# A stick-breaking and forgetting attention block: three loads queued behind the transposing DMA, a second cast tile, and one low part computed ahead of the scan

## The chip, the cores and the metric

The kernel runs on one core of a Trainium2 chip. The metric is device time in microseconds (us) of one execution, as the median of three runs; one further execution was profiled. A core has TensorE (PE, matmul, and PEld for loading its weights), VectorE (DVE), ScalarE (ACT), GpSimd (POOL) and SyncE (SP), which here issues nearly all DMA transfers. Each engine works through its own instructions in order.

## What is computed

One layer of an encoder on a sequence of 512 rows and 2048 columns in float32:

- h = RMSNorm(x); one projection of h gives q, k, v for 16 heads of width 128, and forget gates.
- Eight heads use stick-breaking attention. With z = q k^T / sqrt(128), strictly causal, the weight of key s for query t is exp(log sigmoid(z) + the sum of log sigmoid(-z) over the keys between s and t). That sum is a reversed running sum along each row: a scan.
- Eight heads use forgetting attention: a softmax of z plus a cumulative log-forget bias ("fox" in the code).
- Each head's output o is normalized: o * rsqrt(mean(o^2) + eps) * g.
- x = x + heads @ W_out; x = x + relu(RMSNorm(x) @ W_up)^2 @ W_down; y = RMSNorm(x).

## The kernel before, in words

Every float32 operand of a matmul is split into a high part (rounded by a cast to fp32r on ScalarE) and a low part (the difference, on VectorE), and each product is made of three matmuls (`mm3`, L76 to L79). So each operand costs one cast, one subtraction and room for both parts.

The kernel has a first stage (norm, values), then the attention stage this text is about, then the output projection and the two matrices of the MLP. W_out, W_up and W_down are multiplied with a scheme of seven products, which needs sums of quarters of these matrices; the sums for W_out are made during the attention stage by class `WeightSums` (L952 to L988) and stored to DRAM.

The attention stage has 17 periods, n = 0 to 16, written out by hand as a list of jobs: `plan.at(t, f)` gives job f the time mark t, `plan.run()` calls the jobs in order of their marks, and in this order they stand on each engine. A mark is a place in an order, not a wait. A period has marks of 26.05 (TPER), t = TPER * n; "mark 13.6 of a period" is t + 13.6. In period n three heads are at work:

- Head n is projected: `project` (L205) in four parts, each over eight blocks of 128 rows of W_in, two for q and two for k. Their pieces of W_in (class `Piece`, 512 KB each, tile `wraw`, three in turn) are loaded, cast and subtracted; piece 3 is the last. A piece's tile is free again when its low part is made. Marks on TensorE: 0, 7.35, 14.8, and 20.3 with 23.4.
- Head n-1 has its scores (mark 5.45) and its weights: for fox heads bias, maximum, exponential and scaling; for stick-breaking heads (periods 9 to 16) `start`, `soft`, `maxed` with a causal select on POOL, `scan` (L815: four scans on VectorE and one subtraction), and `weights` (exponential on ScalarE, select on POOL). Then `halves` (L869) parts the upper and lower 16 bits on ScalarE, and `turn_halves` (L873) turns them by a transposing DMA issued from SyncE.
- Head n-2 has its transposed halves joined on ScalarE (`join_halves`, L877, mark 5.4), cast and subtracted (`t_high`, `t_low`), multiplied with the values (`product`, L896, mark 12.85), and normalized: `square` (three operations on ScalarE), `square_low` (L932, VectorE), `norm_sums` (L937 and L938, two matmuls with a matrix of ones on TensorE), `norm_1` (ScalarE), `norm_2` (four operations on VectorE).

Values are loaded for two heads at a time (`load_v`, tile `vr`, one of it), cast (`high_v`) and subtracted (`low_v`).

The sums for W_out come for eight row pairs m. `whole(m)` (m = 0 to 3, periods 1 to 7) loads both sides of a pair, 1 MB each, into a part of the tile `mixed`; `half(m, 0, n)` and `half(m, 1, n)` (m = 4 to 7, called for n = 7, 9, 11, 13 and n = 8, 10, 12, 14) load half of the columns at a time, 512 KB a side, into the one tile `ws`. The first half also has its quarters 0 and 2 cast by `high(i)` into a tile `tboth`, subtracted by `low(i)` and stored to DRAM (`wraws`), and a sixth sum by `high_6`, `low_6` (`whigh`). All three of these casts share the one tile tagged `thi`, so each must wait until the one before is stored. Casts and sums of half(m, 0, n) and half(m, 1, n) fall into period n + 1.

ScalarE, VectorE and TensorE keep this order through the whole stage. SyncE does so up to mark 55.05 only (`free_loads`, L724); after it the framework's planner, which goes by times that it estimates itself, places the transfers in SyncE's queue. The queue is in order: a transfer that has to wait holds all those behind it.

The marks that matter most, on VectorE and ScalarE in a stick-breaking period:

```
for dt, f in zip((12.85, 15.0, 21.7, 23.0, 23.4, 24.8) if late else (12.85, 17.1, 19.2, 20.25, 20.7, 22.05),
                 (H.product, H.square, H.square_low, H.norm_sums, H.norm_1, H.norm_2)):
    plan.at(t + dt, f)
```

(`late` is n > 8 here; the scan stands at 17.0.)

Of the kernel before, what the change touches and what calls it, by code (L numbers as in the profile page):

```python
# [37 lines left out]
def block_kernel(ctx, tc, x, g_attn, w_in, b_f, g_out_sb, g_out_fox, w_out, g_mlp, w_up, w_down, g_final, y):  # L38
# [118 lines left out]
    class Piece:  # L157
# [19 lines left out]
            lows[0] = dve.tensor_tensor(self.lo, self.source(), self.hi.bitcast(F32), op=ALU.subtract)  # L177

        def plan(self, plan, load, cast, low):
            plan.at(load, self.load)  # L180
            plan.at(cast, self.cast)
            plan.at(low, self.low)
            return self

    def q_piece(i, which, half):
        h = order[i]
        c0 = (o0 if h >= NH else 0) + h % NH * P + which * WSB
        return Piece(w_in[half * K8 * P:(half + 1) * K8 * P, c0:c0 + P].rearrange("(a p) c -> p a c", p=P), K8, P)
# [523 lines left out]
    with tc.tile_pool(name="att", bufs=1, side="right", reuse_waits="tile") as at, \  # L712
# [73 lines left out]
        class Head:  # L786
# [13 lines left out]
            def plan_sb(self, plan, t):  # L800
                g = self.h

                def start():
                    self.w = wide("w")
                    act.activation(self.w, self.s, AF.Abs)

                def soft():
                    act.activation(self.w, self.w, AF.Exp, scale=-1.0)
                    act.activation(self.w, self.w, AF.Ln, bias=1.0)

                def maxed():
                    dve.scalar_tensor_tensor(self.w, self.s, 0.0, self.w, op0=ALU.max, op1=ALU.add)
                    causal(self.w, ALU.is_gt, 0.0)

                def scan():  # L815
                    for r in rows(self.w):

                        dve.tensor_tensor_scan(r[:, ::-1], r[:, ::-1], r[:, ::-1], 0.0, op0=ALU.add, op1=ALU.max)
                    dve.tensor_tensor(self.w, self.s, self.w, op=ALU.subtract)

                def weights():
                    act.activation(self.w, self.w, AF.Exp)
                    causal(self.w, ALU.is_gt, 0.0)

                last_ = self.i == 2 * NH - 1
                for dt, f in zip((6.4, 7.7, 10.2, 14.5, 19.2) if last_ else (9.8, 11.0, 13.6, 17.0, 21.7), (start, soft, maxed, scan, weights)):
                    plan.at(t + dt, f)

            def plan_fox(self, plan, t):
# [42 lines left out]

            def turn_halves(self):  # L873
                self.two = wide("pl")
                sp.dma_start_transpose(self.two.bitcast(U16).rearrange("p (b t) -> p b t", t=P), self.one.bitcast(U16))

            def join_halves(self):  # L877
                self.pt = wide("pt")
# [65 lines left out]
            def norm_2(self):  # L944
# [4 lines left out]
                dve.scalar_tensor_tensor(va, sq, -3.0 * P, ra, op0=ALU.add, op1=ALU.mult)  # L949
                dve.scalar_tensor_tensor(mixed[:, self.h, :], self.os, gv, va, op0=ALU.mult, op1=ALU.mult)  # L950

        class WeightSums:  # L952

            def __init__(self, m, ds, place):
# [8 lines left out]
                    sp.dma_start(self.b[:, 2 * s:2 * s + 2], src[:, :, self.ds[0] * NT:self.ds[0] * NT + self.n])  # L963

            def high(self, i):
                self.both = at.tile([P, 2, NT], F32R, tag="thi", name="tboth")
                act.copy(self.both[:, 0], self.q[(0, 2)[i]][:, :NT])

            def low(self, i):
# [20 lines left out]
        def whole(m, t):  # L990
            w = WeightSums(m, (0, 1), lambda: mixed[:, :NH].rearrange("p (q a) n -> p q (a n)", a=2))
            e, o = (t, t + TPER) if m else (TPER, TPER)
            loads = (-4.0 if m == 1 else -15.0, 2.7) if m else (20.5, 20.6)
            highs, lows_, sums_, sixth = ((e + 3.3, o + 3.3), (e + 4.5, o + 4.5), (e + 6.4, e + 16.3, o + 6.4, o + 16.3), (o + 10.7, o + 20.6)) if m else \
                ((e + 4.0, e + 10.0), (e + 5.2, e + 11.0), (e + 6.4, e + 19.2, e + 20.6, e + 21.8), (e + 22.0, e + 24.0))
            for i in range(2):
                plan.at(t + loads[i], w.load, (i,))
                plan.at(highs[i], w.high, i)
                plan.at(lows_[i], w.low, i)
            for i in range(4):  # L1000
                plan.at(sums_[i], w.sum, i)
            plan.at(sums_[1] + 0.1, lambda: w.store(0, 2))
            plan.at(sixth[0], w.high_6)
            plan.at(sixth[1], w.low_6)
            plan.at(sixth[1] + 0.1, lambda: w.store(2, 4))

        def half(m, d, n):
            t = TPER * n
            w = WeightSums(m, (d,), lambda: at.tile([P, 2, 1280], F32, tag="ws", name="ws")
                           .rearrange("p a b -> p (a b)")[:, :4 * NT].rearrange("p (q n) -> p q n", q=4))  # L1010

            def load():
                with tc.issue_after(lows[0].ins):
                    w.load()

            if d == 0:
                jobs = [({7: 8.3, 9: 25.0}.get(n, 13.0), load if n == 7 else w.load)]
                a = (3.3, 4.5, 6.3, 6.35, 16.3, 10.7, 16.35, 20.6, 24.4, 24.9) if n == 7 else (4.3, 5.7, 6.4, 7.1, 7.8, 9.75, 11.3, 12.0, 14.7, 16.3)
                jobs += [(TPER + dt, f) for dt, f in zip(a, (lambda: w.high(0), lambda: w.low(0), lambda: w.sum(0), lambda: w.sum(1), lambda: w.sum(2),
                                                             lambda: w.high(1), lambda: w.low(1), lambda: w.sum(3), w.high_6, w.low_6))]  # L1020
                jobs += [(TPER + a[-1] + 0.1, w.store)]
            else:
                jobs = [(TPER + 3.0 if n == 8 else 20.5, w.load)]
                a = (11.3, 12.0, 16.3, 23.6) if n == 8 else (6.95, 7.65, 8.35, 9.05)
                jobs += [(TPER + dt, lambda j=j: w.sum(j)) for j, dt in enumerate(a)] + [(TPER + a[-1] + 0.1, w.store)]
            for dt, f in jobs:
                plan.at(t + dt, f)
# [22 lines left out]
        for n in range(2 * NH + 1):  # L1050
            t = TPER * n
            i_s, i_o = n - 1, n - 2
            if n < 2 * NH:
                pieces = []
                for a, (which, hf) in enumerate(((0, 0), (0, 1), (1, 0), (1, 1))):
                    if n == 0 and a < 3:
                        pieces.append(first_pieces[a])
                        continue
                    load = (-21.0, -15.0, -14.0, -2.0)[a]
                    if n == 0:  # L1060
                        cast, low, load = 16.3, 18.2, 0.3
                    elif n == 1:
                        cast, low = ((-7.0, -5.0), (-3.0, -2.0), (2.9, 3.9), (8.5, 9.5))[a]
                        load = (-23.0, -19.0, -13.1, -7.5)[a]
                    else:
                        cast, low = ((-12.35, -10.95), (2.3, 3.3), (3.9, 5.2), (9.7, 11.2))[a] if n <= NH else ((-9.25, -3.65), (2.3, 3.3), (3.3, 4.5), (13.6, 15.1))[a]
                        if a == 0 and n == NH + 1:
                            cast, low = -12.35, -10.95
                    pieces.append(q_piece(n, which, hf).plan(plan, t + load, t + cast, t + low))
                marks = [(0, 0, 8, 0.0), (1, 0, 8, 7.35), (2, 0, 8, 14.8), (3, 0, 4, 20.3), (3, 4, 8, 23.4)]  # L1070
                if n == 0:
                    marks = [(2, 0, 2, 16.2), (2, 2, 8, 17.6), (3, 0, 4, 21.6), (3, 4, 8, 24.3)]
# [23 lines left out]
            if 0 <= i_s < 2 * NH:  # L1096
                H = heads[i_s]
                plan.at(t + (5.45 if n < 2 * NH else 4.4), H.scores)
                sb = H.h < NH
                (H.plan_sb if sb else H.plan_fox)(plan, t)  # L1100
                if n < 2 * NH:
                    plan.at(t + (24.7 if sb else 22.0), H.halves)
                    plan.at(t + (24.8 if sb else 22.1), H.turn_halves)
                else:
                    tp = t + 1.45 * 14 + 1.95 - 0.05
                    plan.at(tp, H.turn)
                    plan.at(tp + 1.2, H.p_high)
                    plan.at(tp + 2.5, H.p_low)
                if i_s % 2 == 0 and i_s < 2 * NH - 2:
                    p_ = i_s // 2  # L1110
                    plan.at(t - 12.0 if p_ else t + 3.0, load_v, p_)
                    plan.at(t + (4.3 if sb else 11.3 if p_ else 12.0), high_v, p_)
                    plan.at(t + (5.7 if sb else 24.9 if p_ else 16.35), low_v, p_)
            if 0 <= i_o < 2 * NH - 1:
                H = heads[i_o]
                last_ = i_o == 2 * NH - 2
                for dt, f in zip((11.25, 13.6, 19.3) if last_ else (5.4, 8.5, 9.8), (H.join_halves, H.t_high, H.t_low)):
                    plan.at(t + dt, f)
                if last_:
                    continue  # L1120
                late = n > NH
                for dt, f in zip((12.85, 15.0, 21.7, 23.0, 23.4, 24.8) if late else (12.85, 17.1, 19.2, 20.25, 20.7, 22.05),
                                 (H.product, H.square, H.square_low, H.norm_sums, H.norm_1, H.norm_2)):
                    plan.at(t + dt, f)
        for i, dt in ((2 * NH - 2, 1.0), (2 * NH - 1, 3.0)):
# [979 lines left out]
```

## Time and profile before

| what | us |
|---|---|
| median of three runs | 2039.17 |
| lowest and highest of them | 2039.15, 2040.46 |
| the profiled execution's own time | 2042.29 |
| its span, first to last instruction | 2040.6 |
| TensorE busy in it | 2006.4 |
| granted TensorE clock, mean | 0.995 |
| period 3 (a fox period), from the first matmul of its projection to the next period's | 26.09 |

How to read the profile. Rows of a timeline give the start in us from the span's start, the duration, the engine, the line of the kernel, the operation and its tiles as output<-input; a bracket at the end gives the idle time of the engine before it and what ended that. The engine name SPq stands for SyncE's queue; the duration of a transfer there is that of issuing it, not of the transfer. Matmul durations overlap, as they are pipelined: TensorE starts one about every 0.23 us while a row shows 0.39. The chain of waits is followed back from the last instruction: what it shows are the steps that ended last. Rows of DMA issues give size and median time from issue to landing. The granted clock is 1.00 at full and 0.50 at half speed.

The periods' starts, from the timeline of TensorE (first projection matmul of each head): 200.68 (n = 2), 235.77, 261.86 and so on to 392.33 (n = 9), 418.42, 450.63, 478.98, 508.95, 541.75, 573.54 (n = 15), and 601.45, where the last values begin (n = 16).

### The profile page before, as it was taken

The numbers are of one execution on the slowest core, as the hardware profiler recorded it, in microseconds if no ns is written. First come the engines' busy times: TensorE is split into PE (matmuls) and PEld (weight loads), VectorE is DVE, ScalarE is ACT, GpSimd is POOL, SyncE is SP. The second block draws the span as 40 slices with busy tenths as digits, with TensorE's granted clock in tenths as the row PEclk, the third lists the DMA queues.
The fourth block names the chain that finished last, engine by engine and source line by source line (L and its number), as shares of the span: only waits on it lengthen the run. The fifth ranks groups of instructions, "written<-read, shape, count | busy, mean of one in ns | idle before, by whom it ended". The sixth has DMA issues, their size and how long they took to land.

```text
span 2040.6 us, 27057 instructions
## 1 busy us (share of the span) xinstructions
PE 2006.4 (98%) x10302; PEld 1734.9 (85%) x10302; DVE 1741.2 (85%) x1968; ACT 1201.0 (59%) x1645; POOL 63.6 (3%) x73
## 2 busy tenths in 40 slices
PE   9999899989999999999999999999999999999998
PEld 9998788877778889988888888888888888888887
DVE  7876788787677678899999999998799898888896
ACT  7544666767665566667676676676644444444344
POOL 0000000011010000000000000000000000000003
PEclk9999999999999999999999999999999999999999
DMA  7418877666668882576666667667685674674642
GB/s 257 155 63 255 263 231 213 206 197 183 179 180 277 272 279 95 176 225 191 213 195 209 200 197 221 187 207 258 228 297 207 221 253 175 236 254 173 225 159 89
DMA packets 309426, 423.54 MB, mean 208 GB/s; under 512 B 49408, under 2 KB 205104, under 8 KB 302768
## 3 DMA queue, kind: packets, MB, share of 16 engines
q1 hardware_dynamic: 308544, 419.71, 63.3%
q8 instruction: 81, 1.33, 0.3%
q10 hardware_dynamic: 752, 2.11, 0.3%
q14 instruction: 49, 0.40, 0.1%
HBM read 315.45 MB, written 96.49 MB: 202 GB/s over the span
## 4 chain that ended last, share of the span: by engine, by line
PE 89%; DVE 4%; DMA 3%; ACT 3%; issue 1%; SPq 0%; POOL 0%; ACTq 0%; DVEq 0%
PE psa L1277 11%; PE accd L79 8%; PE accd L78 8%; PE accd L77 8%; PE psa L1275 6%; PE psc L1277 5%; PE accq L77 3%; PE accq L79 3%; PE accq L78 3%; PE psc L1275 3%; PE psb L1277 3%; PE psb L1275 1%; PE m L78 1%; PE m L77 1%; PE m L79 1%; DMA wraws<-tboth 1%
## 5 line engine op out<-in xcount | busy, mean ns | idle before, releaser
L1913 ACT CAST wh<-wd 128x1024 fp32r<-128x1024 f32 x126 | 124.8, 998 | 169.3 <-PE accd L79 54.6
L1799 DVE TENSOR_TENSOR wl<-wu,wh 128x1024 fp32r<-128x1024 f32 x158 | 192.7, 1220 | 12.1 <-ACT wh L1793 12.0
L77 PE MATMUL accq<-hH,wh 128*128 128x512 f32 x512 | 201.7, 394 | 0.0
L79 PE MATMUL accq<-hH,wl 128*128 128x512 f32 x512 | 201.1, 393 | 0.3 <-DVE wl L177 0.3
L78 PE MATMUL accq<-hL,wh 128*128 128x512 f32 x512 | 200.8, 392 | 0.0
L1793 ACT CAST wh<-wu 128x1024 fp32r<-128x1024 f32 x158 | 167.6, 1061 | 44.1 <-issue 28.0
L1277 PE MATMUL psa<-f,wh 128*128 128x512 f32 x720 | 179.1, 391 | 0.0
L78 PE MATMUL accd<-wl,uf 128*128 128x512 f32 x436 | 169.7, 389 | 0.0
L79 PE MATMUL accd<-wh,uf 128*128 128x512 f32 x436 | 169.7, 389 | 0.0
L77 PE MATMUL accd<-wh,uf 128*128 128x512 f32 x436 | 169.6, 389 | 0.0
L1277 PEld LDWEIGHTS psa<-f,wh 128*128 128x128 f32 x720 | 132.4, 188 | 25.5
L1920 DVE TENSOR_TENSOR wl<-wd,wh 128x1024 fp32r<-128x1024 f32 x126 | 144.0, 1151 | 10.9 <-ACT wh L1913 10.9
L1913 ACT CAST wx<-wd 128x1024 fp32r<-128x1024 f32 (+1 forms) x82 | 80.8, 994 | 106.5 <-PE accd L79 41.9
L1634 DVE TENSOR_TENSOR m<-m,accd 128x1024 f32<-128x1024 f32 x84 | 102.2, 1217 | 46.3 <-PE accd L79 46.3
L79 PEld LDWEIGHTS accq<-hH,wl 128*128 128x128 f32 x512 | 96.8, 189 | 21.7 <-DVE wl L177 1.2
L78 PEld LDWEIGHTS accq<-hL,wh 128*128 128x128 f32 x512 | 97.0, 189 | 19.5
L77 PEld LDWEIGHTS accq<-hH,wh 128*128 128x128 f32 x512 | 97.2, 190 | 19.0
L77 PE MATMUL accd<-wx,uf 128*128 128x512 f32 x284 | 110.6, 389 | 0.0
L79 PE MATMUL accd<-wx,uf 128*128 128x512 f32 x284 | 110.6, 389 | 0.0
L78 PE MATMUL accd<-wx,uf 128*128 128x512 f32 x284 | 110.6, 389 | 0.0
L1275 PEld LDWEIGHTS psa<-f,wl 128*128 128x128 f32 x720 | 96.0, 191 | 5.3
L1275 PE MATMUL psa<-f,wl 128*128 128x256 f32 x720 | 98.3, 283 | 0.0
(443 smaller groups left out, 5135.3 us busy)
## 6 DMA issues: line engine op xcount, KB each, us to landing
wu<-in_w_up_dram SPq DMA_DIRECT2D x60, 1024.0 KB, 6.7
ufd<-st SPq DMA_DIRECT2D x98, 512.0 KB, 3.9
wd<-in_w_down_dram SPq DMA_DIRECT2D x48, 1024.0 KB, 8.7
uf<-ufd SPq DMA_DIRECT2D x42, 1024.0 KB, 8.0
wraw<-in_w_in_dram SPq DMA_DIRECT2D x68, 512.0 KB, 5.6
wo<-wsums SPq DMA_DIRECT2D x28, 512.0 KB, 4.5
q<-in_w_in_dram SPq DMA_DIRECT2D x32, 384.0 KB, 5.4
wd<-in_w_down_dram SPq DMA_DIRECT2D x16, 768.0 KB, 5.8
```

The lines of the kernel that those rows point to most:

```text
L77: pe.matmul(out, sh, mh, start=first, stop=False, skip_group_check=True)
L78: pe.matmul(out, sh, ml, start=False, stop=False, skip_group_check=True)
L79: return pe.matmul(out, sl, mh, start=False, stop=last, skip_group_check=True)
L1275: ins = pe.matmul(ps[:, 2 * P:], lo[:, a, :], f_parts(p, a)[0], start=False, stop=last, skip_group_check=True)
L1277: ins = pe.matmul(ps, hi[:, a, :], f_both(p, a), start=a == PAIRS[0] and p in (1, 5), stop=last, skip_group_check=True)
L1634: dve.tensor_tensor(M[p][:, :, db, :], M[p][:, :, db, :], ps, op=ALU.add)
L1793: act.copy(rooms[k][0], srcs[k])
L1799: lows[0] = dve.tensor_tensor(lo, srcs.pop(k), hi.bitcast(F32), op=ALU.subtract)
L1913: act.copy(rooms[k + 3][0], srcs[k + 3])
L1920: dve.tensor_tensor(rooms[k + 2][1], srcs.pop(k + 2), rooms[k + 2][0].bitcast(F32), op=ALU.subtract)
```

## The change

- `turn_halves` keeps its transposing DMA, and a new function `load_behind` issues a load inside `tc.issue_after(...)` of that DMA: the planner must place it in SyncE's queue behind the transposition. It is used for piece 3 of heads 3 to 15 (at t - 0.5 instead of t - 2.0) and for the load of the second halves of the W_out sums (mark 25.5 instead of 20.5, or 29.05 for n = 8).
- In the first halves the second cast `high(1)` goes into the tile of the value loads (`vr`) instead of `thi`. The value loads of stick-breaking periods stand at t - 7.0 instead of t - 12.0.
- In periods 9 to 16 `square_low` stands at 16.9, ahead of the scan, instead of 21.7, `norm_sums` at 20.25 instead of 23.0, `norm_1` at 20.7 instead of 23.4, ahead of `weights` (22.0 instead of 21.7), and `norm_2` at 24.4 instead of 24.8.
- The second halves' four sums stand at 8.35, 9.05, 11.3, 12.0 (before: 6.95 to 9.05, and 11.3 to 23.6 for n = 8). In period 8 the first half's third sum, second low part, last sum and sixth stand earlier; the load for n = 9 stands at 13.0 instead of 25.0.
- For m = 1 the first load stands at mark 0.5 of period 2 instead of 4.0 before it, its cast at 10.7 instead of 3.3, its low part at 11.15, and its first two sums at 16.3 and 24.9.

```diff
         def plan(self, plan, load, cast, low):
-            plan.at(load, self.load)
+            if load is not None:
+                plan.at(load, self.load)
...
                 last_ = self.i == 2 * NH - 1
-                for dt, f in zip((6.4, 7.7, 10.2, 14.5, 19.2) if last_ else (9.8, 11.0, 13.6, 17.0, 21.7), (start, soft, maxed, scan, weights)):
+                for dt, f in zip((6.4, 7.7, 10.2, 14.5, 19.2) if last_ else (9.8, 11.0, 13.6, 17.0, 22.0), (start, soft, maxed, scan, weights)):
...
-                sp.dma_start_transpose(self.two.bitcast(U16).rearrange("p (b t) -> p b t", t=P), self.one.bitcast(U16))
+                now["turn"] = sp.dma_start_transpose(self.two.bitcast(U16).rearrange("p (b t) -> p b t", t=P), self.one.bitcast(U16))
...
+        def load_behind(w):
+            with tc.issue_after(now["turn"].ins):
+                w.load()
...
             def high(self, i):
-                self.both = at.tile([P, 2, NT], F32R, tag="thi", name="tboth")
+                self.both = at.tile([P, 2, NT], F32R, tag="vr" if i and self.n == NT else "thi", name="tboth")
...
-            loads = (-4.0 if m == 1 else -15.0, 2.7) if m else (20.5, 20.6)
-            highs, lows_, sums_, sixth = ((e + 3.3, o + 3.3), (e + 4.5, o + 4.5), (e + 6.4, e + 16.3, o + 6.4, o + 16.3), (o + 10.7, o + 20.6)) if m else \
+            loads = (0.5 if m == 1 else -15.0, 2.7) if m else (20.5, 20.6)
+            highs, lows_, sums_, sixth = ((e + 3.3, o + 3.3), (e + 4.5, o + 4.5), (e + 6.4, e + 16.3, o + 6.4, o + 16.3), (o + 10.7, o + 20.6)) if m > 1 else \
+                ((e + 10.7, o + 3.3), (e + 11.15, o + 4.5), (e + 16.3, e + 24.9, o + 6.4, o + 16.3), (o + 10.7, o + 20.6)) if m else \
...
             if d == 0:
-                jobs = [({7: 8.3, 9: 25.0}.get(n, 13.0), load if n == 7 else w.load)]
-                a = (3.3, 4.5, 6.3, 6.35, 16.3, 10.7, 16.35, 20.6, 24.4, 24.9) if n == 7 else (4.3, 5.7, 6.4, 7.1, 7.8, 9.75, 11.3, 12.0, 14.7, 16.3)
+                jobs = [(8.3 if n == 7 else 13.0, load if n == 7 else w.load)]
+                a = (3.3, 4.5, 6.3, 6.35, 16.3, 10.7, 11.15, 17.0, 18.85, 20.6) if n == 7 else (4.3, 5.7, 6.4, 7.1, 7.8, 9.75, 11.3, 12.0, 14.7, 16.3)
...
             else:
-                jobs = [(TPER + 3.0 if n == 8 else 20.5, w.load)]
-                a = (11.3, 12.0, 16.3, 23.6) if n == 8 else (6.95, 7.65, 8.35, 9.05)
+                jobs = [(25.5, lambda: load_behind(w))]
+                a = (8.35, 9.05, 11.3, 12.0)
...
-                    pieces.append(q_piece(n, which, hf).plan(plan, t + load, t + cast, t + low))
+                    w = q_piece(n, which, hf)
+                    if a == 3 and n > 2:
+                        plan.at(t - 0.5, load_behind, w)
+                        load = None
+                    pieces.append(w.plan(plan, load and t + load, t + cast, t + low))
...
-                    plan.at(t - 12.0 if p_ else t + 3.0, load_v, p_)
+                    plan.at(t - (7.0 if sb else 12.0) if p_ else t + 3.0, load_v, p_)
...
-                for dt, f in zip((12.85, 15.0, 21.7, 23.0, 23.4, 24.8) if late else (12.85, 17.1, 19.2, 20.25, 20.7, 22.05),
+                for dt, f in zip((12.85, 15.0, 16.9, 20.25, 20.7, 24.4) if late else (12.85, 17.1, 19.2, 20.25, 20.7, 22.05),
                                  (H.product, H.square, H.square_low, H.norm_sums, H.norm_1, H.norm_2)):
```

## The prediction

> **What bounds the kernel now.** I read the page first, then the stretches, then chain, waits and timeline of the slow ones. The page:
>
> ```profile
> span 2040.6 us, 27057 instructions
> PE 2006.4 (98%) x10302; PEld 1734.9 (85%) x10302; DVE 1741.2 (85%) x1968; ACT 1201.0 (59%) x1645; POOL 63.6 (3%) x73
> PE 89%; DVE 4%; DMA 3%; ACT 3%; issue 1%; SPq 0%; POOL 0%; ACTq 0%; DVEq 0%
> ```
>
> TensorE is the bound; only time in which it stands still or runs at half clock can be won. The change lies in the attention part. I cut that at the first projection matmul (accq) of each head, as the timeline gives it, and asked for busy time in those stretches. Columns: stretch, length, busy PE, PEld, DVE, ACT, POOL, granted clock, DMA share, GB/s.
>
> ```profile
> core 0: us, PE busy (x) PEld busy (x) DVE busy (x) ACT busy (x) POOL busy (x), PEclk, DMA share, GB/s
> 200.68:235.77 35.09, 28.50 (x127) 23.89 (x125) 22.03 (x33) 17.61 (x24) 2.13 (x2) 0.90 0.90 274
> 235.77:261.86 26.09, 26.09 (x126) 22.11 (x125) 21.67 (x33) 18.73 (x25) 2.00 (x2) 1.00 0.74 227
> 418.42:450.63 32.21, 26.96 (x127) 22.02 (x125) 23.51 (x28) 20.61 (x22) 3.51 (x4) 1.00 0.72 217
> 450.63:478.98 28.35, 26.93 (x126) 22.03 (x125) 22.16 (x26) 20.20 (x20) 3.06 (x4) 1.00 0.79 231
> 478.98:508.95 29.97, 26.71 (x127) 21.96 (x125) 23.20 (x28) 20.98 (x22) 3.51 (x4) 1.00 0.58 168
> 508.95:541.75 32.80, 29.43 (x127) 24.53 (x125) 22.21 (x26) 20.64 (x20) 3.06 (x4) 0.90 0.74 197
> 541.75:573.54 31.79, 28.28 (x127) 23.10 (x125) 24.68 (x30) 21.92 (x22) 3.51 (x4) 0.95 0.52 149
> 573.54:601.45 27.91, 26.74 (x127) 22.03 (x125) 19.59 (x23) 17.86 (x18) 3.06 (x4) 1.00 0.63 175
> ```
>
> The second row (period 3) is clean: TensorE busy throughout, 26.09 us. Against it period 2 loses 9.00, and periods 10 to 15 lose 6.12, 2.26, 3.88, 6.71, 5.70 and 1.82: 35.5 us in all, clock dips included. That is the whole purse. Which waits fill it, by the list of waits of 180 to 640 us (total, times, longest) and the chain:
>
> ```profile
> PE ssq L938 <- DVE pl L932: 9.5, 3, 3.2
> ACT tboth L967 <- DMA wraws<-tboth: 17.2, 5, 6.3
> ```
> ```profile
> 452.05 7.26 DMA pl<-pt
> ...
> 486.04 6.57 DMA wraws<-tboth
> ...
> 510.39 9.27 DMA pl<-pt
> ...
> 573.40 8.38 DMA pl<-pt
> ```
>
> Three things end last: the norm sums on TensorE wait for `square_low`, which stands behind the scan (9.5 us, periods 10, 12, 14); the second `tboth` waits until the first is stored; and the transposing DMA at the end of the even periods takes 7.26, 9.27 and 8.38 us. SyncE's queue shows what the last meets, and the odd end at 480 shows it undisturbed:
>
> ```profile
> 449.14 1.21 SPq L963 DMA_DIRECT2D ws<-in_w_out_dram  x2
> 450.44 0.55 SPq L163 DMA_DIRECT2D wraw<-in_w_in_dram  x1
> 452.05 5.14 SPq L875 DMA_TRANSPOSE pl<-pt  x1
> ...
> 459.39 3.10 ACT L879 COPY pt<-pl 128x2560 uint16<-128x2560 uint16 x1 [2.86 <-DMA pl<-pt]
> ...
> 480.43 2.56 SPq L875 DMA_TRANSPOSE pl<-pt  x1
> ...
> 484.63 3.12 ACT L879 COPY pt<-pl 128x2560 uint16<-128x2560 uint16 x1
> ...
> 492.67 0.62 ACT L967 CAST tboth<-ws 128x512 fp32r<-128x512 f32 x1 [3.62 <-DMA wraws<-tboth]
> ...
> 505.11 0.68 DVE L932 TENSOR_TENSOR pl<-ph,pl 128x512 fp32r<-128x512 f32 x1
> ```
>
> Three loads of 512 KB go out in the 3 us before the slow transposition. The quick one has the join (L879) start 4.20 us after its issue, without a wait.
>
> **The change, part by part.** *Loads tied behind the transposition* (piece 3 of heads 3 to 15, the second half's two `ws` loads). They are the three in front of 452.05. What a transposition takes with loads behind it I bound from both sides: 4.2 us with none, and from a fox period with a 1 MB load right behind it:
>
> ```profile
> 260.22 2.53 SPq L875 DMA_TRANSPOSE pl<-pt  x1
> ...
> 262.84 0.53 SPq L963 DMA_DIRECT2D mixed<-in_w_out_dram  x1
> ...
> 265.74 3.11 ACT L879 COPY pt<-pl 128x2560 uint16<-128x2560 uint16 x1
> ```
>
> The join did not wait, so it had landed within 5.52. I take 4.85, the middle. By the Trainium skill, "DMA: Bandwidth & Descriptors", section "Two DMAs through the same engine are not ordered", descriptors of one queue start in order, so loads behind should cost nothing; by that it would be 4.2 and the sum below some 4 us better. A later load on its side: piece 3 is cast at mark 13.6 of its period, issued now near 3; hidden, and if it came 8 us later ScalarE's cast would hold the join loop us for us.
>
> *Second cast in the value tile.* The 3.62 us wait of period 12 goes (for m from 4; the whole pairs keep the one tile). The tile is needed for the value load only at mark 19 of the same period; that load moves from 12 to 7 ahead of its period, and its cast is at 4.3, eleven us later: nothing on the path.
>
> *`square_low` ahead of the scan.* VectorE's row of 0.68 now lies on the loop from join to next transposition. The join loop per pair of periods, by the rows above: odd, 459.39 to 480.43 = 21.04, plus 0.68 = 21.72; even, 484.63 to 510.39 = 25.76, less 3.62, plus 0.68 = 22.82; with two transpositions of 4.85 it is 54.24 against 52.18 of TensorE (52.94 at 4.2, 55.58 at 5.52). So the loop becomes the bound by 2.06 per pair, 6.2 in three pairs, less the slack it starts with. The slack: the join of period 12 comes 5.65 after the start and costs nothing, that of period 11 comes 8.76 after and costs
>
> ```profile
> 465.37 0.39 PE L78 MATMUL o<-pl,vh 128*128 128x256 f32 x1 [1.14 <-DVE pl L886]
> ```
>
> 1.14, so the limit is 7.6 and the slack 2.0. Left: 4.2 us (0.3 to 8.2).
>
> One rule speaks against this move. POOL's causal select runs just ahead of the scan:
>
> ```profile
> 498.71 2.14 POOL L778 TENSOR_SCALAR_AFFINE_SELECT w<-w 128x256 f32<-128x256 f32 x2 [20.67 <-DVE w L812]
> 506.63 1.37 POOL L778 TENSOR_SCALAR_AFFINE_SELECT w<-w 128x256 f32<-128x256 f32 x2 [5.78 <-ACT w L822]
> ```
>
> Beside VectorE's subtractions it takes 2.14, alone 1.37: they do slow one another, by 0.77. The Trainium skill, "SBUF — State Buffer", section "Who interferes with whom", has it that a VectorE instruction with two SBUF inputs and a GpSimd one that reads SBUF exclude each other for the whole instruction; `square_low` has two such inputs. By that rule up to 0.77 more per period would go onto the loop, six times, 4.6 us; by the rows two subtractions stand beside the select already, so I take nothing.
>
> *Norm sums and `norm_1` earlier.* TensorE now reaches the sums at mark 20.25 instead of 23. `square_low` would end where the scan of period 12 began, 4.6 us before 505.11, less 3.62, plus 0.68: 18.2 after 478.98. So 9.5 us of TensorE waiting go, with 2 us to spare; if the loop slips by more, the wait returns. The new wait: `norm_1` stands ahead of `weights` on ScalarE and waits for TensorE; behind it stand weights, select, halves, transposition. Sums done at 20.7, two activations of 0.65: 22.0; the scan's end is 23 in period 12 by the same reckoning, so 1 us of cover. `norm_2`, 0.4 earlier, stays last in its period: nothing.
>
> *The half pair's sums* (odd periods) move from 6.95–9.05 to 8.35–12.0, two ahead of `t_low`, two behind. Their `ws` loads now follow the transposition:
>
> ```profile
> ws<-in_w_out_dram SPq DMA_DIRECT2D x16, 512.0 KB, 5.2
> ...
> wsums<-ws SPq DMA_DIRECT2D x8, 1024.0 KB, 6.5
> ```
>
> Issued at 2.56 and 3.2 after the transposition's issue they land near 7.8 and 8.4; sums of 0.7 each end near 9.2, and `t_low` could begin at 4.85 + 3.12 + 1.27 = 9.2. Between nothing and 1.3 each; I take 0.5, 1.5 us in all. With the cover gone (a load that waits for the old tile's store first) each us late is a us lost. The first half's load of period 9 moves up 12 marks, and period 8's casts up 5.5: both off the path.
>
> *Pair 1's first load and casts* (period 2).
>
> ```profile
> 197.69 2.33 ACT L871 COPY pt<-w 128x2560 uint16<-128x2560 uint16 x1 [1.83 <-DVE w L856]
> ...
> 203.29 0.34 SPq L963 DMA_DIRECT2D mixed<-in_w_out_dram  x1
> 203.75 6.37 SPq L875 DMA_TRANSPOSE pl<-pt  x1
> 210.22 0.52 SPq L984 DMA_DIRECT2D whigh<-thi  x1
> ...
> 213.44 0.62 ACT L967 CAST tboth<-mixed 128x512 fp32r<-128x512 f32 x1 [8.64 <-DMA whigh<-thi]
> ...
> 214.91 3.04 ACT L879 COPY pt<-pl 128x2560 uint16<-128x2560 uint16 x1
> ```
>
> The halves are done at 200.02, the transposition goes out at 203.75 behind a waiting 1 MB load, the `whigh` store behind that, and a cast that waits for the store holds ScalarE until 213.44 and with it the join. Load and cast both move behind the join. Then: issue 200.05, landed by 205.6 (5.52), join 4.9 after the period's start, inside 7.6: all 9.0 come back. What is late next is the moved cast at mark 10.7, ahead of period 2's softmax; a miss of 2 us there meets the fox periods' slack.
>
> Sum: purse 35.5, less 4.2 (loop), less 1.5 (sums): 29.8. The profiled execution took 2042.29 (span 2040.6), 3.1 above the median of 2039.17; taking the gain from the median gives **2009.4**.
>
> **The rivals.** *Other loads slide in front.* After mark 55.05 SyncE's order is the planner's; only the named loads are tied. If untied pieces or stores precede the even transpositions, these keep their mean of 8.30: 57.69 per pair, 5.51 over, 16.5 in three, less 2.0, plus 1.5: gain 19.5, 2019.7. That is also the case that the ties do not do what they say. For it: stores of 1 MB a period pass the same queue; against: at 480.43 the order was clean.
>
> *`ws` late.* If these loads wait for a store and land 4 us later, VectorE holds `t_low` in three odd periods: 12 more, gain 17.8, 2021.4. For it: both halves share one tile; against: the store goes out at mark 16.4 and takes 6.5, done by 23.
>
> *Exclusion at the select*, as above: 4.6 more, 2014.0.
>
> *Slower.* The tie touches every head from 3 on. If the planner puts a load that waits (for a tile still being stored) between the transposition and piece 3, ScalarE's in-order queue holds cast, softmax and halves in each of 13 periods. It decides from 29.8 / 13 = 2.3 us a period; at 4 us, 2061. For it: in period 2 one waiting load on this queue cost 9 us; against: issued behind a fox period's transposition (260.22 + 2.53, 0.9 into its period) piece 3 has nearly 9 us until its cast at mark 9.7, where a load of its size takes 5.2.
>
> **How the numbers follow.** Forecast 55% (its own range 2003 to 2016: loop at its bounds), exclusion 10%, other loads 13%, `ws` late 10%, slower 9%, mishaps that cancel 3%. All but the last two are faster by over 0.2% (4 us; about what a measurement of this kernel can tell). The range runs from 2002 (the purse, and 1.7 for the neighbouring periods) to 2028 (above the two late cases).
>
> **What would show it.** Right: transpositions of periods 10, 12, 14 landing within 5.5 us, with `ws` and piece 3 issued behind; no wait of `tboth` for `wraws` from period 8 on; no wait of ssq for `square_low`; period 2 near 26. Wrong: joins later than 7.6 after the start, VectorE idle before the `ws` sums, ScalarE idle before `norm_1`. The forecast falls if the clean 26.09 of the fox periods grows, or if SyncE's order puts a waiting load ahead of the transposition.

## The result, and the profile after

The changed kernel takes 2012.23 us (median of four runs, 2011.52 to 2012.47) against 2039.81 of the kernel before in the same comparison (four runs, 2039.15 to 2040.46). The ratio is 0.9864, 95% interval 0.9847 to 0.9881: 27.6 us less, by the medians. The forecast was 2009.4, so direction and size came out. The profile shows that three terms of the sum did not, and that they nearly cancelled, which is luck.

The page of the changed kernel, the lines that answer to those of before (span; busy time; shares of the chain that ended last):

```profile
span 2010.4 us, 27058 instructions
PE 1997.9 (99%) x10302; PEld 1730.5 (86%) x10302; DVE 1738.8 (86%) x1968; ACT 1202.2 (60%) x1645; POOL 58.3 (3%) x73
PE 96%; DVE 1%; DMA 1%; ACT 0%; SPq 0%; issue 0%; ACTq 0%; DVEq 0%
```

TensorE's share of the chain went from 89% to 96%, and its busy time fell by 8.5 us although it runs the same 10302 matmuls. All of that lies in periods 10 to 15 (165.05 us busy before, 156.56 after, by the stretches), most of it in the two whose granted clock was 0.90 and 0.95 and is now 1.00. The profiled execution took 2012.10, which is the median almost to the tenth. Before, the profiled one stood 2.5 above its median.

The same stretches as in the prediction, cut again at the first projection matmul of each head (stretch, length, busy PE, PEld, DVE, ACT, POOL, granted clock, DMA share, GB/s). The last row is a part of the first:

```profile
core 0: us, PE busy (x) PEld busy (x) DVE busy (x) ACT busy (x) POOL busy (x), PEclk, DMA share, GB/s
200.78:232.01 31.23, 28.28 (x127) 23.21 (x125) 21.16 (x33) 17.36 (x23) 0.82 (x2) 0.95 0.86 262
232.01:258.10 26.09, 26.09 (x126) 22.11 (x125) 21.67 (x33) 18.74 (x25) 2.00 (x2) 1.00 0.79 252
414.66:440.76 26.10, 26.10 (x127) 22.11 (x126) 22.36 (x28) 20.65 (x22) 3.06 (x4) 1.00 0.72 217
440.76:466.85 26.09, 26.09 (x127) 22.11 (x125) 22.28 (x26) 20.77 (x20) 2.45 (x4) 1.00 0.74 227
466.85:492.94 26.09, 26.09 (x126) 22.11 (x125) 22.35 (x28) 20.67 (x22) 3.06 (x4) 1.00 0.74 217
492.94:519.04 26.10, 26.10 (x127) 22.11 (x125) 22.29 (x26) 20.78 (x20) 2.45 (x4) 1.00 0.74 227
519.04:545.13 26.09, 26.09 (x127) 22.11 (x125) 22.36 (x28) 20.64 (x22) 3.06 (x4) 1.00 0.65 197
545.13:571.22 26.09, 26.09 (x126) 22.10 (x125) 21.14 (x25) 19.80 (x19) 2.45 (x4) 1.00 0.68 206
224.00:228.00 4.00, 3.50 (x9) 2.73 (x9) 2.31 (x4) 2.61 (x4) 0.00 (x0) 0.58 0.05 14
```

Periods 10 to 15 (the six rows from 414.66) are all clean: the 26.49 us that they had lost came back whole. Period 2 (the first row) is 31.23 long and still loses 5.14 of its 9.00. The value stage n = 16 begins at 571.22 instead of 601.45, 30.23 earlier, and the span is shorter by 30.2: nothing else moved.

### The profile page after: what moved, and what is told of

It is laid out like the page before. It is cut to its first block, busy times and chain, and to the rows that moved or that the text cites. A ratio compares the mean times of both kernels' runs of the same rounds, so it can differ in the third digit from the quotient of the medians.

```text
span 2010.4 us, 27058 instructions
## 1 busy us (share of the span) xinstructions
PE 1997.9 (99%) x10302; PEld 1730.5 (86%) x10302; DVE 1738.8 (86%) x1968; ACT 1202.2 (60%) x1645; POOL 58.3 (3%) x73
## 4 chain that ended last, share of the span: by engine, by line
PE 96%; DVE 1%; DMA 1%; ACT 0%; SPq 0%; issue 0%; ACTq 0%; DVEq 0%
PE psa L1287 11%; PE accd L78 8%; PE accd L79 8%; PE accd L77 8%; PE psa L1285 6%; PE psc L1287 5%; PE accq L77 5%; PE accq L79 5%; PE accq L78 5%; PE psc L1285 3%; PE psb L1287 3%; PE psb L1285 1%; PE m L78 1%; PE m L77 1%; PE m L79 1%; PE accoa L79 1%
## 5 line engine op out<-in xcount | busy, mean ns | idle before, releaser
L77 PE MATMUL accq<-hH,wh 128*128 128x512 f32 x512 | 200.8, 392 | 0.0
L77 PE MATMUL accd<-wh,uf 128*128 128x512 f32 x436 | 169.4, 389 | 0.0
L1930 DVE TENSOR_TENSOR wl<-wd,wh 128x1024 fp32r<-128x1024 f32 x126 | 144.1, 1152 | 10.6 <-ACT wh L1923 10.6
L77 PEld LDWEIGHTS accq<-hH,wh 128*128 128x128 f32 x512 | 96.6, 189 | 19.0
L77 PE MATMUL accd<-wx,uf 128*128 128x512 f32 x284 | 110.5, 389 | 0.0
```

The costliest lines, as they stand in the source:

```text
L77: pe.matmul(out, sh, mh, start=first, stop=False, skip_group_check=True)
L1930: dve.tensor_tensor(rooms[k + 2][1], srcs.pop(k + 2), rooms[k + 2][0].bitcast(F32), op=ALU.subtract)
```

## What the queue and the loop look like now

SyncE's queue and the join at the start of period 11, from the timeline (start, duration, engine, line, operation, tiles; the idle time before it in brackets), and the median time of a transposition from issue to landing in 400 to 640 us, from the list of transfers:

```profile
441.67 2.55 SPq L876 DMA_TRANSPOSE pl<-pt  x1
444.31 1.21 SPq L968 DMA_DIRECT2D ws<-in_w_out_dram  x2
445.57 4.28 SPq L163 DMA_DIRECT2D wraw<-in_w_in_dram  x3
445.89 3.11 ACT L880 COPY pt<-pl 128x2560 uint16<-128x2560 uint16 x1 [0.28 <-DMA pl<-pt]
...
pl<-pt SPq DMA_TRANSPOSE x7, 4.2
```

The two `ws` loads and three pieces now go out behind the transposition, and the join starts 4.22 after its issue. The undisturbed transposition of before took 4.20. The loads behind it cost nothing that can be seen, where I had taken 4.85; the rule of the Trainium skill, "DMA: Bandwidth & Descriptors", section "Two DMAs through the same engine are not ordered" (descriptors of one queue start in order), would have put it at 4.2, and here the trace agrees with it.

Period 2, again by the timeline:

```profile
199.47 4.99 SPq L876 DMA_TRANSPOSE pl<-pt  x1
204.56 0.51 SPq L989 DMA_DIRECT2D whigh<-thi  x1
205.12 0.42 SPq L163 DMA_DIRECT2D wraw<-in_w_in_dram  x1
205.65 0.66 SPq L992 DMA_DIRECT2D wsums<-mixed  x1
206.40 0.46 SPq L968 DMA_DIRECT2D mixed<-in_w_out_dram  x1
206.63 3.12 ACT L880 COPY pt<-pl 128x2560 uint16<-128x2560 uint16 x1 [1.46 <-DMA pl<-pt]
...
215.42 0.62 ACT L972 CAST tboth<-mixed 128x512 fp32r<-128x512 f32 x1 [3.42 <-DMA mixed<-in_w_out_dram]
...
223.59 0.50 PE L938 MATMUL ssq<-pl,onesr 128*128 128x512 f32 x1 [2.45 <-ACT pl L930]
224.59 0.78 PE L939 MATMUL ssq<-pl,onesr 128*128 128x512 f32 x1 [0.50 <-DVE pl L933]
```

The transposition goes out at 199.47 instead of 203.75, near the 200.05 worked out. It takes 7.16 us and not 5.52, as a store of 1 MB (`wsums`, at 198.24) and 0.25 MB (`cb`, at 198.65) went out just ahead of it. The join starts at 206.63 instead of 214.91. But pair 1's cast (`tboth<-mixed`, mark 10.7) now waits 3.42 us on ScalarE for its 1 MB load, which is issued at 206.40 behind a store, a piece and a 1 MB store. The cast stands in ScalarE's order ahead of the softmax and the squares of the norm; these come late, and TensorE stands 2.95 us (2.45 + 0.50) at the norm sums. What follows runs at a granted clock of 0.58 from 224 to 228. Idle 31.23 - 28.28 = 2.95, and busy time 28.28 - 26.09 = 2.19 too long from the clock: 5.14.

## The experiments

In the expectations, theory A is the prediction's working, in which the ties carry most of what periods 10 to 15 win; theory B, its rival, gives the ties little. C and D ask of pair 1 whether the place of its cast or the order of the transfers is the cause. E and F stand for two readings of the norm part: E, that it is worth the waiting it takes away; F, that this waiting was only where a late loop showed. The median of the kernel before was 2037.14 us beside e1 to e4 (2036.62 to 2038.94), 2036.24 beside e5, e6, e8 and e9 (2034.98 to 2038.36), and 2038.32 beside the rest (2035.05 to 2041.19). Each ratio is to the kernel before on the same chip.

### The ties: both away, and one of two

`e1_untied`: the marks stay, the tie goes.

```diff
         def load_behind(w):
-            with tc.issue_after(now["turn"].ins):
+            with ExitStack():
                 w.load()
```

> The changed kernel with all its marks, but the loads are not tied behind the transposing DMA (the planner places them freely). Theory A (join, cast and transposition lie on one loop, so each part undone costs its own wait): the two ws loads and piece 3 are queued ahead of the even transpositions again, which then land after about 8 us instead of 4.25; 3.75 x 3 = 11 us, less some 2 us of slack: periods 11, 13 and 15 lengthen by 9 us together, about 2021 us. Theory B (the norm part alone carries the gain of periods 10 to 15): the slow transpositions are hidden, at most 2 us more, 2012 to 2014 us.

2022.81 us (2022.32 to 2023.92), ratio 0.9932 (0.9909 to 0.9954). Periods 11, 13 and 15 are 30.46, 31.73 and 28.64 long, the others of 10 to 15 are 26.1. The start of period 11 in its timeline:

```profile
439.32 1.21 SPq L968 DMA_DIRECT2D ws<-in_w_out_dram  x2
440.62 0.55 SPq L163 DMA_DIRECT2D wraw<-in_w_in_dram  x1
441.26 6.36 SPq L876 DMA_TRANSPOSE pl<-pt  x1
...
449.70 3.10 ACT L880 COPY pt<-pl 128x2560 uint16<-128x2560 uint16 x1 [4.75 <-DMA pl<-pt]
```

Without the tie the planner puts the three loads ahead again, and the transposition takes 449.70 - 441.26 = 8.44 (8.93 and 8.47 in the next two even periods). That costs 10.6 us by the medians, 11.8 by the spans of the profiled executions. A holds, B falls: the ties are the largest single part.

`e8_ws_tied` leaves piece 3 free, `e9_piece_tied` leaves the `ws` loads free.

```diff
 e8:
-                        plan.at(t - 0.5, load_behind, w)
+                        plan.at(t - 0.5, w.load)
 e9:
-                jobs = [(25.5, lambda: load_behind(w))]
+                jobs = [(25.5, w.load)]
```

> The changed kernel with the ws loads tied and piece 3 free: it stands ahead of every transposition, 0.5 MB. If bytes ahead of the transposition delay it (0.5 MB, about 1.5 us, less the time that the piece was issued earlier) the transpositions land after 4.25 to 5.5 us; the loop's slack of some 2 us takes that up: periods 10 to 15 lengthen by 0 to 3 us together, 2012 to 2015 us. If it is the count of loads or their place that matters, it lengthens as untied, by 10 us.

> The changed kernel with piece 3 tied and the two ws loads free: in SyncE's queue they stand right ahead of the transpositions of periods 10, 12, 14, 1 MB. By bytes ahead: these land after about 7 us, periods 11, 13, 15 lengthen by some 2.5 each less slack, 6 to 8 us in all, 2018 to 2020 us. If piece 3 is what matters, no change, 2012 us.

e8: 2008.70 us (2008.60 to 2008.79), ratio 0.9862 (0.9842 to 0.9881), all of periods 10 to 15 at 26.09. e9: 2013.02 us (2012.76 to 2013.28), ratio 0.9883 (0.9863 to 0.9903), periods 11, 13 and 15 at 26.35, 27.49 and 27.52. The timeline of e8 at the start of period 11, then that of e9:

```profile
434.86 0.37 SPq L163 DMA_DIRECT2D wraw<-in_w_in_dram  x1
...
438.45 2.39 SPq L876 DMA_TRANSPOSE pl<-pt  x1
```

```profile
437.04 1.21 SPq L968 DMA_DIRECT2D ws<-in_w_out_dram  x2
438.98 4.05 SPq L876 DMA_TRANSPOSE pl<-pt  x1
...
445.08 3.10 ACT L880 COPY pt<-pl 128x2560 uint16<-128x2560 uint16 x1 [2.17 <-DMA pl<-pt]
```

Left free, the piece goes out 3.6 us before the transposition and is out of its way: the transposition takes 4.25, as with both ties. The free `ws` loads stand right ahead of it, and it takes 6.10 (6.18 and 6.10 later), a loss of 3.1 us in the three periods, half of the 6 to 8 expected. So the tie of `ws` is the one that is needed; that of the piece matters only where `ws` is free too. In bytes just ahead of the transposition: none 4.2, 1 MB 6.1, 1.5 MB 8.4 to 8.9 us here. How long ahead they went out seems to count as well. The half megabyte 3.6 us ahead cost nothing; and with 1.5 MB the kernel before had 7.3 us where the first load went out 2.9 us ahead, and 8.5 and 9.4 where it was 2.0 and 2.2.

### The second cast's tile

`e2_one_tile`:

```diff
-                self.both = at.tile([P, 2, NT], F32R, tag="vr" if i and self.n == NT else "thi", name="tboth")
+                self.both = at.tile([P, 2, NT], F32R, tag="thi", name="tboth")
```

> The changed kernel with the second cast of the first halves back in the tile of the first. Theory A: the cast waits for the store of the first again, 3 to 4 us in each of periods 10, 12, 14 on the join loop; 3.6 x 3 less 2 of slack = 9 us, about 2021 us. Theory B: hidden, at most 2 us more, 2012 to 2014 us.

2018.39 us (two runs, 2016.13 and 2020.66), ratio 0.9907 (0.9876 to 0.9937): 6.2 us above the changed kernel. The profiled execution, the longer of the two, has periods 10 to 15 at 26.48, 27.48, 27.35, 26.76, 27.53 and 29.73, 8.8 us in all above clean ones. Its timeline, and its waits in 410 to 580 us (total, times, longest):

```profile
481.16 0.62 ACT L972 CAST tboth<-ws 128x512 fp32r<-128x512 f32 x1 [2.81 <-DMA wraws<-tboth]
...
ACT tboth L972 <- DMA wraws<-tboth: 7.9, 3, 2.8
```

The wait comes back in three periods, 2.8 us at most, and each puts the loop of join, cast, scan and transposition behind TensorE. This part too does what the prediction said of it. In this execution the 7.9 us waited show whole in the time; the other one, not profiled, was 4.5 us shorter.

### The norm part: back, alone, and back without the ties

`e3_norm_back` undoes it in the changed kernel. `e10_untied_norm_back` does the same on top of e1. `e7_norm_alone` is the kernel before with the norm part alone (the same lines the other way round).

```diff
 e3, e10 (e7: the reverse, on the kernel before):
-(9.8, 11.0, 13.6, 17.0, 22.0), (start, soft, maxed, scan, weights)
+(9.8, 11.0, 13.6, 17.0, 21.7), (start, soft, maxed, scan, weights)
...
-(12.85, 15.0, 16.9, 20.25, 20.7, 24.4) if late
+(12.85, 15.0, 21.7, 23.0, 23.4, 24.8) if late
```

> The changed kernel with square_low, norm_sums, norm_1, norm_2 and weights of periods 9 to 16 at their old marks. Theory A: TensorE waits for square_low behind the scan again, about 3 us in each of several periods, 9 to 14 us with the half clock, about 2021 to 2026 us. Theory B: nearly the whole gain of periods 10 to 15 goes, 20 us or more, 2032 us or above.

> The kernel before with nothing but the marks of square_low, norm_sums, norm_1, norm_2 and weights changed. Theory E (TensorE's 9.5 us of waiting at the norm sums was a cost of its own): some 9 us less. Theory F (it was a symptom: while join, cast and transposition run late, TensorE waits in one place or another for the same loop, and the 0.68 us of square_low lengthen that loop): the wait at the sums goes and the waits at the product grow by as much; within 3 us of the kernel before.

> The changed kernel with its loads untied and the norm part back at its old marks. With the loads tied, undoing the norm part cost nothing; untied alone cost 10 to 12 us (periods 11, 13, 15 longer by 4.4, 5.6 and 2.5). Theory E: the norm part's share shows once the loop is late, 5 us or more above the untied kernel, about 0.996 of the kernel before. Theory F: as the untied kernel, 0.993, or a little less time, since the 0.68 us are off the loop.

e3: 2010.85 us (two runs, 2010.71 and 2010.98), ratio 0.9869 (0.9841 to 0.9898). Neither A nor B had that. Its stretch of period 10 stays clean, like the five after it:

```profile
413.30:439.39 26.09, 26.09 (x127) 22.10 (x125) 23.19 (x28) 20.60 (x22) 3.50 (x4) 1.00 0.76 217
```

`square_low` is behind the scan again, and yet TensorE does not wait for it: with the loop on time the scan is done early enough.

e7: 2040.64 us (eight runs, 2036.55 to 2043.02) against 2038.32 (thirteen), ratio 1.0006 (0.9995 to 1.0017): nothing. TensorE's waits in the attention part (390 to 606 us; total, times, longest), first of the kernel before, then of e7:

```profile
PE ssq L938 <- DVE pl L932: 9.5, 3, 3.2
PE o L77 <- ACT ph L883: 3.6, 3, 2.2
```

```profile
PE o L77 <- ACT ph L883: 8.7, 4, 2.8
PE ssq L938 <- DVE pl L932: 2.3, 3, 0.9
```

The waits at the sums fall by 7.2, and those of the product for the joined and cast weights (o L77) rise by 5.1; the six periods take 181.76 us in place of 183.03. The loop is as late as before, and TensorE waits for it one step earlier. F holds, E falls. e10: 2019.17 us (two runs, 2017.95 and 2020.38), ratio 0.9910 (0.9890 to 0.9930), against 0.9932 (0.9909 to 0.9954) of e1: no loss, as F had it. In the profiles periods 10 to 15 take 164.1 us in all against 169.1 in e1, but that does not show that the old place of `square_low` is the better one where the loop is late. The planner made another order of loads here, with a piece well ahead of the `ws` loads in periods 10 and 12 (SyncE's queue and the join at the start of period 11, by the timeline):

```profile
438.70 1.21 SPq L968 DMA_DIRECT2D ws<-in_w_out_dram  x2
440.42 4.85 SPq L876 DMA_TRANSPOSE pl<-pt  x1
...
447.36 3.09 ACT L880 COPY pt<-pl 128x2560 uint16<-128x2560 uint16 x1 [2.34 <-DMA pl<-pt]
```

The three slow transpositions take 6.94, 7.02 and 7.99 us where e1 had 8.44, 8.93 and 8.47. That is 3.9 of the 5.0 us, and what the 0.68 us of `square_low` cost on a late loop stays open.

### Pair 1: back, its cast later, its load later

`e4_pair1_back` gives pair 1 its old marks. `e5_cast_late` takes the changed kernel and moves the cast, its low part and its first sum to 19.0, 19.95 and 20.5 of period 2. `e6_load_late` also moves pair 1's loads.

```diff
 e5:
-                ((e + 10.7, o + 3.3), (e + 11.15, o + 4.5), (e + 16.3, e + 24.9, o + 6.4, o + 16.3), (o + 10.7, o + 20.6)) if m else \
+                ((e + 19.0, o + 3.3), (e + 19.95, o + 4.5), (e + 20.5, e + 24.9, o + 6.4, o + 16.3), (o + 10.7, o + 20.6)) if m else \
 e6, on top of it:
-            loads = (0.5 if m == 1 else -15.0, 2.7) if m else (20.5, 20.6)
+            loads = (6.0 if m == 1 else -15.0, 6.1 if m == 1 else 2.7) if m else (20.5, 20.6)
```

> The changed kernel with the load, cast and sums of pair 1 at their old marks. Both theories: only period 2 changes, from 31.23 back to about 35.1 us, so 3.9 us more, about 2016 us; if the move of pair 1 did nothing of itself and period 2 gained through the tie of piece 3, it stays near 31.

> The changed kernel with pair 1's first cast at mark 19.0 of period 2 (behind the norm's squares) instead of 10.7, its low part at 19.95 and first sum at 20.5. In the changed kernel ScalarE waits 3.42 us for the load at this cast, and then 0.90 for a piece at the next one; softmax and squares queue behind both and TensorE's norm sums come 2.95 late, with half clock behind that. Theory C (the cast's place is the cause): the softmax starts some 1.8 us earlier, held only by the piece; norm sums about 1 us late and no half clock: period 2 falls from 31.2 to about 28, 3 us less, 2009 us. Theory D (the transfers are the cause, since 3.3 MB stand in SyncE's queue behind the transposition): the next piece still lands at the same time and holds the same softmax; period 2 near 29.5 or above, 2010.5 us.

> As the run before, and pair 1's two loads at marks 6.0 and 6.1 of period 2, so that one more piece of W_in stands ahead of the 1 MB load in SyncE's queue. Theory C: nothing more than the run before, about 28 us for period 2. Theory D: the piece lands 2.8 us earlier (1 MB at 0.36 MB per us), the softmax starts at its mark, period 2 comes to 26.1 to 27 us, 2007 to 2008 us.

e4: 2014.85 us (two runs, 2014.60 and 2015.10), ratio 0.9889 (0.9860 to 0.9918); e5: 2008.27 (2007.11 to 2008.56), ratio 0.9858 (0.9842 to 0.9875); e6: 2006.04 (2005.59 to 2006.81), ratio 0.9849 (0.9834 to 0.9864). Only period 2 differs between them. Its stretch in e4, then in e5 with the next thing that waits, then in e6 with the same instruction:

```profile
200.08:234.53 34.45, 28.33 (x126) 23.69 (x125) 21.97 (x33) 17.46 (x24) 2.13 (x2) 0.90 0.84 261
```

```profile
200.14:228.08 27.94, 26.69 (x127) 22.02 (x125) 21.81 (x34) 17.79 (x24) 0.81 (x2) 1.00 0.91 293
...
216.76 1.05 ACT L170 CAST wh<-wraw 128x1024 fp32r<-128x1024 f32 x1 [4.46 <-DMA wraw<-in_w_in_dram]
```

```profile
213.96 1.05 ACT L170 CAST wh<-wraw 128x1024 fp32r<-128x1024 f32 x1 [2.61 <-DMA wraw<-in_w_in_dram]
```

34.45 with the old marks, 31.23 with the change's, 27.94 with the cast behind the softmax, 26.09 with the load behind one more piece. In e5 the waiting cast of pair 1 is gone, and the next instruction to hold ScalarE is the cast of a piece whose load is queued behind pair 1's megabyte; e6 puts one of the pieces ahead of it, the wait shrinks from 4.46 to 2.61, and TensorE no longer stands. So the place of the cast and the order of the transfers both count.

`after_again` and `e6_again` repeat the changed kernel and e6 on one chip.

> The changed kernel once more, beside the next one on the same chip, since chips differ by a few us: about 0.986 of the kernel before.

> The kernel of pair 1 loaded and cast late, once more: its period 2 was 26.09 us against 28.9 to 31.2 of kernels with pair 1 as in the changed kernel. All theories: 3 to 5 us below the changed kernel on the same chip, 0.983 to 0.985 of the kernel before.

2012.01 us (2011.36 to 2013.61), ratio 0.9874 (0.9857 to 0.9890), and 2006.05 (2005.82 to 2006.13), ratio 0.9845 (0.9831 to 0.9860). e6 stands 6.0 us below the changed kernel and beats both. Its period 2:

```profile
199.64:225.74 26.10, 26.10 (x127) 22.12 (x126) 21.11 (x33) 17.18 (x23) 0.81 (x2) 1.00 0.93 297
```

In the changed kernel repeated, period 2 was 32.93 long and the rest clean. With pair 1 as in the change the profiled period 2 was between 28.93 (e8) and 32.93 long, so this one period makes most of what differs between those kernels; e8's 3.5 us below the changed kernel is 2.3 from there.

## Why the prediction was right, and where it was wrong

*Loads tied behind the transposition: right, and mis-sized.* Transpositions of periods 10, 12 and 14 landing within 5.5 us with the loads behind them was the sign asked for; they land in 4.22 to 4.29. The term "loop residue 4.2" measured 0. By e8 and e9 the tie of `ws` did this, and that of piece 3 was not needed. The join loop of a pair of periods now takes 52.13: two transpositions of 4.26 and 4.22 (issued at 415.22 and 441.67, joins at 419.48 and 445.89), 419.48 to 441.67 = 22.19 and 445.89 to the next issue at 467.35 = 21.46. I had 54.24 from 4.85 twice, 22.82 and 21.72. TensorE needs 52.18, so the loop keeps step. How much room it has the 52.13 does not say, as it holds waits for TensorE too: ScalarE's order now has `norm_1` ahead of `weights`, and `norm_1` waits for the sums. The timeline of period 11:

```profile
461.07 1.49 DVE L820 TENSOR_TENSOR w<-s,w 128x1280 f32<-128x1280 f32 x1
461.61 0.69 ACT L942 ACTIVATE ra<-ssq,eps 128x512 f32<-128x512 f32 x1 [2.92 <-PE ssq L939]
...
462.87 1.26 ACT L823 ACTIVATE w<-w 128x1280 f32<-128x1280 f32 x1
```

"ScalarE idle before `norm_1`" was to be a sign of being wrong. It came, with 2.92 us, and cost next to nothing: the scan's subtraction ends at 462.56 and `weights` start 0.3 later, so the 1 us of cover was used up and hardly more.

*Second cast in the value tile: right.* e2 gives it 6.2 us by the medians, against the 3.62 of one period that I had read.

*Norm part: wrong as a cause.* "So 9.5 us of TensorE waiting go" came true in the trace (no wait of ssq for `square_low` is left in periods 10 to 15), but it is no gain of the move: e3 has none of these waits with the old marks, and e7 has the move and no gain. I had read the wait that ended last as the place of the cause. The sum was not harmed, since the purse counted the whole loss of a period, whatever wait it ended in, and not one wait after the other. A slip stands in the same place: 505.11 less 4.6, less 3.62, plus 0.68 is 18.6 after 478.98 and not 18.2, so 1.7 us were to spare and not 2.

*Exclusion at the select (a rival, 10%).* `square_low` beside the select takes longer. The timeline of the changed kernel:

```profile
429.83 2.14 POOL L779 TENSOR_SCALAR_AFFINE_SELECT w<-w 128x256 f32<-128x256 f32 x2 [17.00 <-DVE w L813]
431.63 0.89 DVE L933 TENSOR_TENSOR pl<-ph,pl 128x512 fp32r<-128x512 f32 x1
```

0.89 for 0.68: 0.2 us and not 0.77, and no wait of TensorE follows from it. The rule of the Trainium skill ("SBUF — State Buffer", section "Who interferes with whom") shows in its direction. Whether one blocks the other for a whole instruction these rows do not test, as the select ends at 431.97, 0.34 us after `square_low` starts. The price of 0.77 had a wrong reading in it: the select of 1.37 us in the kernel before was not alone, since its timeline has beside it

```profile
506.85 0.89 DVE L746 TENSOR_TENSOR ul<-qf,uh 128x512 fp32r<-128x512 f32 x1
```

*Half pair's sums: residue 1.5 forecast, 0 measured.* VectorE does wait for the late loads, as the list of waits of the changed kernel says (180 to 640 us):

```profile
DVE ws L980 <- DMA ws<-in_w_out_dram: 7.3, 6, 2.7
```

7.3 us in six waits, none of which reaches TensorE: all six periods are clean. This was to be a sign of being wrong too. The condition of the rival "`ws` late" (12 us), a load that waits for a store, did not come about: in period 11 both loads go out right behind the transposition, and the waiting sums start 7.0 and 8.3 us after its issue (448.69 and 449.96), where 7.8 and 8.4 were worked out.

*Pair 1: the step that failed.* "All 9.0 come back" was wrong: 3.86 did. The join came 5.85 after the period's start, later than the 4.9 worked out and inside 7.6. What failed is the sentence after it, "a miss of 2 us there meets the fox periods' slack". The miss was 3.42, since the load has a store, a piece and another store ahead of it in a full queue, where I had priced the transposition alone; and the softmax, which I had named as next in line, has no such slack: TensorE stood 2.95 us behind it and then lost 2.19 to the clock. e5 and e6 bring back the rest.

*The base.* I took the gain, worked out in an execution of 2042.29, from the median of 2039.17. In that execution the gain was 2042.29 - 2012.10 = 30.2, beside 29.8 forecast; by the medians it is 27.6. The errors above are +5.7 (4.2 and 1.5 that did not remain) and -5.1 (period 2), which leaves the 2.8 us between 2009.4 and 2012.23 almost wholly to this: the long profiled execution had more to lose than the median one. Taking the gain from its own execution would have given 2012.5.

*Not tried apart:* the marks of the half sums, the earlier load of period 9 and the earlier casts of period 8; and which of the old waits makes the kernel before vary by 6 us from run to run, where e6 varies by 1.2.

## What to carry to other kernels

Where engines in fixed orders make a loop (here join, cast, scan, transposition), add up the loop and compare it with the bound engine's period; a wait at one of its ends says that the loop is late, and removing that wait alone only moves it. On an in-order queue, put bulk loads behind the transfer that the loop needs and not ahead of it: behind it they were free, right ahead of it each half megabyte cost about 1 to 1.7 us, and half a megabyte 3.6 us ahead cost nothing. An early cast of a late load holds all that stands behind it on its engine; place it by the bytes queued ahead of its load, and when it is mended look for the next load in the same queue.

## What the runs showed of the hardware

The transposing DMA's time followed the bytes just ahead of it in its queue: 4.2 us with none, 6.1 to 7.2 with 1 to 1.25 MB, and 7.2 (e7) to 9.4 with 1.5 MB. It followed those behind it not at all. The time that SyncE needs to issue it grew with the bytes ahead (2.55, 4.05 and 6.36 us in the rows above).

A TensorE gap of about 3 us can cost a second time, by the clock, or not. In the kernel before, a stand of 3.23 us ahead of the norm sums at 505.85 was followed by 3.15 us at a granted clock of 1.00, and one of 3.23 ahead of 568.86 by 5.14 us at 0.67; in the changed kernel one of 2.45 and 0.50 was followed by 0.58. Equal gaps with and without the dip agree with a window that runs freely of the kernel, as the Trainium skill has it ("TensorE: Matmul & The Clock Gate", Part 1). The traces show the steps of such a window. In the attention stage of the kernel before, the granted clock is 0.50 from 217.70 to 224.53, from 524.90 to 531.73 and from 569.27 to 572.68, and 1.00 elsewhere: 6.83, 6.83 and 3.41 us, with starts 90 times and 13 times 3.413 us apart. On this grid the second stand of 3.23 us lies almost whole in one step, with TensorE busy for 0.41 of 3.41 us (stretches of the kernel before, columns as above):

```profile
565.86:569.27 3.41, 0.41 (x2) 0.37 (x3) 3.38 (x4) 0.97 (x1) 0.00 (x0) 1.00 0.99 362
569.27:572.68 3.41, 3.41 (x10) 2.64 (x9) 3.25 (x5) 3.14 (x4) 1.37 (x2) 0.50 0.04 16
```

The first is divided over two steps, busy for 1.62 and 1.99. In the changed kernel TensorE was busy for 0.54 us of the step ahead of the dip. So these runs agree with this much: the clock was halved after a step that was mostly idle, and not after the same idle time divided over two.

In period 2 of the changed kernel the dip made the 2.95 us of waiting cost 5.14, 1.7 times their length.
